# Query and gate transposes by DMA from DRAM in a hybrid retention and attention layer

## The chip, the core and the metric

The kernel runs on one core of one Trainium2 chip. Such a core has five engines that run side by side, each with its own list of instructions: TensorE (PE, the matrix engine), VectorE (DVE), ScalarE (ACT), GpSimd (POOL) and SyncE (SP). Here SP issues all transfers but one, in order, and sixteen DMA engines carry them out. SBUF is the memory on the core with 128 partitions, PSUM the banks that TensorE writes, DRAM the large memory outside. The metric is the device time of one execution in microseconds (us), lower is better.

## What is computed

One decoder layer, with x of 2048 tokens by 1024 channels, all in float32. After an RMS norm one projection gives the columns of two groups of heads and a gate for each group:

```python
h = rms_norm(x, norm_w)
rq, rk, rv, rg, sq, sk, sv, sg = split(h @ w_in)         # 256 256 512 512 512 128 128 512
# A: retention, 4 heads, chunks of 128 tokens
scores = (qc @ kc.T) * decay ;  intra = scores @ vc       # qc, kc with rotary phase
state = chunk_decay * state + (kc * zeta).T @ vc ;  cross = (qc * xi) @ state_before
ro = group_norm(intra + cross) * ret_norm_w * silu(rg)
# B: attention over a window of 128 keys, 8 query heads, 2 key heads
q, k = rms_norm(sq, q_norm_w), rms_norm(sk, k_norm_w)
logits = q @ kband.T / 8 + bias                           # the chunk's keys and the previous chunk's
so = softmax([logits, sink])[..., :-1] @ vband * silu(sg)
out = x + concat([ro, so]) @ w_out
```

## The kernel before, in words

The tokens are cut into 16 chunks of 128, taken as 8 pairs. The two projections run as four stages of block products: stage 1 gives the columns of sq, sk and sv, stage 2 those of rq, rk and rv, stage 3 the gates rg and sg, stage 4 is the output projection. Each stage forms, for each pair, a 2 by 2 block product in seven products in place of eight (the numbers 1 to 7 in `STEPS`), so that there are 4 x 7 x 8 = 224 products. Each float32 operand is split into a high and a low part (`split`: ACT makes the high part, DVE the low one), and a product is twelve matmuls, three for each of four slices of the inner dimension. They write the tiles called `acc`. TensorE's other results are called `m`.

Attention (`window`, `attend`, `values`) runs between the products of stages 2 and 3, a chunk at a time: load queries (`aq`) and keys (`akv`) from DRAM, multiply by their norm factors (`qn`, `kn`), transpose the key (`turn k`) and the four 128-column blocks of the queries (`turn q`) on TensorE against the identity (`ident`), copy them from PSUM on ACT (`ks`, `qT`), logits, softmax, four transposes of the weights for each key head (`turn weights`, `pT`), and for each pair of chunks the product with the values. The values are read from DRAM into `vn`, `vs` and `vd`, each of 128 partitions by four shifted runs of 128 columns, in quarters of 32 partitions. `retention` does the same for its heads. Both groups' outputs (`so`, `ro`) go to DRAM.

The gates (`gates`, `gate(n, c, ...)`: n = 0 for retention, 1 for attention, c the chunk) come from the products of stage 3. The gate of retention for an even chunk is put into DRAM (`g_dram`) and read back, at a due time of `GATE[0] + p * GATE[1]` for pair p; the others are used as they come. With n = 0 the output `go` is multiplied by the gate, transposed on TensorE in four blocks (`turn gated`, 16 chunks x 4) and copied back from PSUM on ACT (`mixed`). With n = 1 the gate itself is transposed by `turn_by_dma`, while `so` is already transposed. That function exists because the transposing DMA works on 16-bit elements: ACT first puts the low and the high half words of all 512 columns apart (`apart`, 1024 columns of uint16), SP issues a transposing DMA from SBUF to SBUF (`turned`), and ACT puts the halves together again. `go` then goes into stage 4 as an operand.

The order of the instructions is made by a planner, `Program.emit`, when the kernel is built. Each operation has a due time, counted in products, and costs for its engine (time taken, time to the result). The planner walks through time, takes for each engine the operation that can start first by these costs, and emits it. So on each engine, and on SP's list of transfers ("Q"), the order is fixed at build time, and on the chip an instruction waits at its place for what it needs; what stands behind it on that engine waits too. Buffers of 128 by 512 (tag `k`) are shared by all, in groups with a limit (`SHARE`; the group of `apart` and `turned` has 6).

Every operation is recorded through one helper, so all rows of the profile bear its line, L377, and are told apart by their tiles: `m<-ident,qn` are the query transposes, `m<-ident,go` those of the gated outputs, `m<-ident,kn` the keys', `m<-ks,qT` the logits, `acc<-w,x` the products.

Of the kernel before, what the change touches and what calls it, by code (L numbers as in the profile page):

```python
# [310 lines left out]
LOG = None  # L311


def dve(n, two=False, lat=0.08):
# [34 lines left out]
def dma(kb, issue=0.45):  # L349
    return {"Q": (0.45 + kb / 1024, 2.6, issue)}  # L350


# [28 lines left out]
def layer(ctx, tc, xt, xfirst, xtok, nw, w_in, w_rn, qkw, sinks, biasg, rope, dmask, gpow, w_out, out):  # L381
# [35 lines left out]

    def scratch(shape, name, n):
        t = dram.tile([n, *shape], F32, name=name)
        return [Buf(name=name, ap=t[i]) for i in range(n)]  # L420
# [13 lines left out]
    def store(dst, b, due, kbytes=256, of=lambda t: t):  # L434
        op(dma(kbytes), lambda e: e.dma_start(dst(), of(b())), [b], [dst], due, label=f"store {b.name}")

    def f(t):
# [384 lines left out]
    def retention(at):  # L822
# [4 lines left out]
        for c in range(NCH):  # L827
# [3 lines left out]
            v0, v1 = (Part(v, lambda t, s=s: t[:, s]) for s in (slice(0, 256), slice(256, 512)))  # L831
            load(a0, rq_dram[0][c], due - 3, 192, also=(a,))
            load(a1, rq_dram[1][c], due - 3, 64, also=(a,), of=lambda t: t[:, 0:128])
            load(rp, given(rope[c].rearrange("p s c -> p (s c)")), due - 3)
            load(v0, rq_dram[1][c], due - 3, 128, also=(v,), of=lambda t: t[:, 128:384])
            load(v1, aq_dram[1][c], due - 3, 128, also=(v,), of=lambda t: t[:, 256:512])
            for j, r in enumerate((rstd_all, rsq_all)):

                def go(e, rp=rp, j=j, r=r, c=c):
                    t = rp().rearrange("p (s c) -> p s c", s=2)[:, :, j * P : (j + 1) * P]  # L840
                    e.activation(t, t, AF.Copy, scale=r()[:, c : c + 1])

                op({"A": act(256, 0.09)}, go, [rp, r], [rp], due - 2, label="scale rope")

            tcos, tsin, qk = kb("tcos", "ret"), kb("tsin", "ret"), kb("qk", "ret")
            for i, t in enumerate((tcos, tsin)):

                def go(e, t=t, i=i, a=a, rp=rp):
                    h = "p (h c) -> p h c"
                    e.tensor_tensor(  # L850
                        t().rearrange(h, h=2),
                        a().rearrange(h, h=2),
                        rp().rearrange("p (s c) -> p s c", s=2)[:, i : i + 1, :].to_broadcast([P, 2, 256]),
                        ALU.mult,
                    )

                op(both(512), go, [a0, a1, rp], [t], due, label="rotary", also=(a,))

            for i, alu in enumerate((ALU.subtract, ALU.add)):
# [10 lines left out]

                op(both(256), go, [tcos, tsin], [qk], due + 0.1, label="rotary sum")

            pt, qkT = ps(), kb("qkT", "ret")

            def go(e, pt=pt, qk=qk):
                for i in range(4):
                    e.transpose(pt()[:, i * P : (i + 1) * P], qk()[:, i * P : (i + 1) * P], ident())

            op(turns(4), go, [qk, ident], [pt], due + 0.2, "small", label="turn qk")

            op({"A": act(512)}, lambda e, pt=pt, qkT=qkT: e.activation(qkT(), pt(), AF.Copy), [pt], [qkT], due + 0.3,
               label="qkT")
            halves = (slice(0, 64), slice(64, 128))
# [132 lines left out]
    def window(at):  # L1016
# [44 lines left out]
    def values_from(c, rows, part, whole, name, due):  # L1061


        first = c * P + rows
        source = [akv_dram[k] for k in range(-1, NCH) if first < (k + 2) * P and first + P > (k + 1) * P]
        src = akv_rows[first : first + P, 128:256].rearrange("(u p) d -> p u d", p=32)
        op(
            dma(64, 0.63), lambda e: e.dma_start(part().rearrange("p (u d) -> p u d", d=P), src), source, [part], due - 4,
            label="load " + name, also=(whole,),
        )  # L1070

    def values(c, held, due, d, differences):
# [4 lines left out]
        n, s = kb("vn", "att"), kb("vs", "att")  # L1077
        parts = []
# [5 lines left out]
        for k, (place, seen, whole) in enumerate(((differences[0], parts[0], n), (differences[3], parts[7], s))):  # L1084
            values_from(c + k, P, place, d, "vd", due)
            op(
                both(512), lambda e, place=place, seen=seen: e.tensor_tensor(place(), place(), seen(), ALU.subtract),
                [place, seen], [place], due + 1, label="vd", also=(d, whole),
            )
# [5 lines left out]
        def go(e):  # L1095
# [9 lines left out]
            for u in range(4):  # L1105
                for g, r in enumerate((L, H)):
                    for k, rows in enumerate((L, H)):
# [5 lines left out]
                        )  # L1113

        reads = [*parts, *differences, *held[0][0], *held[1][0], *held[0][2], *held[1][2]]
        op(f32(512, 3.2), go, reads, pavs, due + 2, "both", label="values", also=(n, s, d, *own))
        for k in range(2):
            so = kb("so", "att")
            op({"A": act(512)}, lambda e, so=so, k=k: e.activation(so(), pavs[k](), AF.Copy), [pavs[k]], [so], due + 2.1,
               label="so")  # L1120
            store(so_dram[c + k], so, due + 2.2)

# [45 lines left out]
    def attend(c, a, b, fac, facs, due, bias_t, ks_t, nsnk, held):  # L1168
# [11 lines left out]

        op(both(512), go, [a, facs], [qn], due, label="qn")

# [14 lines left out]

        def go(e):
            for i in range(4):
                e.transpose(pq()[:, i * P : (i + 1) * P], qn()[:, i * P : (i + 1) * P], ident())  # L1200

        op(turns(4), go, [qn, ident], [pq], due + 0.2, "small", label="turn q")
        qT = kb("qT", "att")

# [75 lines left out]
        for g in range(KVH):  # L1280
            pm, own = pms[g], owns[g]
            pp, pT = ps(), kb("pT", "att")

            def go(e, pp=pp, pm=pm):
                for j in range(GRP):
                    e.transpose(pp()[:, j * P : (j + 1) * P], pm()[:, j * P : (j + 1) * P], ident())

            op(
                turns(4), go, [*weights_of[g], *weights_of[2 + g], ident], [pp], due + 1.3 + 0.3 * g, "small",
                label="turn weights", also=(pm,),  # L1290
            )
            op({"A": act(512)}, lambda e, pT=pT, pp=pp: e.activation(pT(), pp(), AF.Copy), [pp], [pT], due + 1.4 + 0.3 * g,
               label="pT")

# [9 lines left out]

            op({"G": (0.61, 0.7, True)}, go, [pT], [part], due + 1.5 + 0.3 * g, label="own", also=(own,))
            pTs.append(pT)
# [15 lines left out]
    mixes = {}  # L1322

    def turn_by_dma(t, due):


        apart, turned = kb("apart", "turned"), kb("turned", "turned")
        words = lambda x: x.bitcast(U16).rearrange("p (c h) -> p h c", h=2)
        planes = lambda x: x.bitcast(U16).rearrange("p (h c) -> p h c", h=2)
        op(  # L1330
            {"A": act(1024)}, lambda e: e.activation(planes(apart()), words(t()), AF.Copy), [t], [apart], due,
            label="apart",
        )
        op(
            {"Q": (1.4, 3.0, 0.45)},
            lambda e: e.dma_start_transpose(
                turned().bitcast(U16).rearrange("p (j r) -> p j r", r=P), apart().bitcast(U16)
            ),
            [apart], [turned], due, label="turn by dma",
        )  # L1340
        op(
            {"A": act(1024)}, lambda e: e.activation(words(t()), planes(turned()), AF.Copy), [turned], [t], due + 0.1,
            label="together",
        )

    def gate(n, c, due, g):
# [14 lines left out]
        else:  # L1361
# [96 lines left out]
RET = (107.0, 2.8)  # L1458
GATE = (150.0, 1.2)

# [97 lines left out]
```

## Time and profile before

| | us |
|---|---|
| median of 3 runs (709.15 to 710.41) | 709.81 |
| the profiled execution, whole | 709.88 |
| its span, first to last instruction | 708.0 |
| PE busy | 702.2 |
| DVE busy | 606.9 |
| ACT busy | 471.9 |
| share of the sixteen DMA engines | 67.5% |

The profile is of one execution. A row of a group reads: line, engine, operation, tile written, tiles read, shape, count, then the busy time of all, the mean length of one in ns, and the time the engine stood idle ahead of them with what ended it. In a row of waits stand who waited, on what, the sum, how often and the longest. A row of issued transfers gives the destination, the source, the size and the time from issue to landing. "SPq" is SP's list of transfers. The tile views of a transfer give the time for which one instruction holds SP (shortest, median, longest) and its time to landing.

### The profile page before, as it was taken

What the parts mean: (1) busy time and instruction counts of PE and PEld (TensorE: products, weight loads), DVE (VectorE), ACT (ScalarE), POOL (GpSimd) and SP (SyncE); (2) the same over time, 40 slices, a digit from 0 to 9 for tenths busy, and PEclk for the clock granted to TensorE, in tenths of its full rate; (3) what the DMA queues carried; (4) which work ended last, traced back from release to release, by engine and by line L of the source; (5) the groups of instructions that cost most, each with busy time, mean ns of one, the idle gap of its engine ahead of it and who ended that gap; (6) DMA issues with size and microseconds to landing.
All of it is one profiled execution on the core that took longest, in us unless ns stands there. A gap on an engine that the chain in (4) does not pass through costs nothing.

```text
span 708.0 us, 15295 instructions
## 1 busy us (share of the span) xinstructions
PE 702.2 (99%) x5324; PEld 603.3 (85%) x5324; DVE 606.9 (86%) x1458; ACT 471.9 (67%) x1103; POOL 43.8 (6%) x75
## 2 busy tenths in 40 slices
PE   9999999999999999999999999999999999999998
PEld 7888888889999999998888888888888878888886
DVE  6999877877997977799999979998699989997862
ACT  7666966655795548788588667789999976250500
POOL 1000000025110001002001010000000000000000
PEclk9999999999999999999999999999999999999999
DMA  8978939968545557998977738292999951324722
GB/s 322 358 263 294 404 123 316 313 230 276 183 132 169 198 172 213 357 302 257 335 223 251 208 114 290 71 333 100 303 341 235 256 128 60 103 91 131 256 103 90
DMA packets 118924, 157.66 MB, mean 223 GB/s; under 512 B 28736, under 2 KB 57408, under 8 KB 118848
## 3 DMA queue, kind: packets, MB, share of 16 engines
q1 hardware_dynamic: 118704, 156.69, 67.5%
q8 instruction: 42, 0.69, 0.4%
q14 instruction: 34, 0.28, 0.1%
q10 hardware_dynamic: 144, 0.00, 0.0%
HBM read 110.44 MB, written 42.01 MB: 215 GB/s over the span
## 4 chain that ended last, share of the span: by engine, by line
PE 97%; DVE 2%; issue 0%; DMA 0%; SPq 0%; ACT 0%
PE acc L377 80%; PE m L377 17%; DVE w L377 1%; DVE x L377 1%; DVE t L377 0%; DMA res<-in_xtok 0%; DVE res L377 0%; DVE go L377 0%; SPq L377 0%; ACT x L377 0%; DVE none L377 0%
## 5 line engine op out<-in xcount | busy, mean ns | idle before, releaser
L377 PE MATMUL acc<-w,x 128*128 128x512 f32 (+1 forms) x2700 | 598.5, 378 | 1.1 <-DVE x L377 0.8
L377 PEld LDWEIGHTS acc<-w,x 128*128 128x128 f32 x2700 | 491.1, 188 | 82.0 <-issue 2.7
L377 DVE TENSOR_TENSOR x<-x 128x512 fp32r<-128x512 f32 (+2 forms) x220 | 145.4, 681 | 16.4 <-ACT x L377 15.9
L377 ACT ACTIVATE x<-x 128x512 fp32r<-128x512 f32 (+1 forms) x187 | 112.1, 617 | 7.0 <-DVE x L377 2.6
L377 ACT ACTIVATE w<-w 128x512 fp32r<-128x512 f32 (+1 forms) x72 | 41.2, 603 | 38.1 <-DMA w<-in_w_out 17.8
L377 DVE TENSOR_TENSOR w<-w 128x512 fp32r<-128x512 f32 (+3 forms) x96 | 62.5, 669 | 2.9 <-ACT w L377 2.9
L377 DVE TENSOR_TENSOR s<-acc,s 128x512 f32<-128x512 f32 (+1 forms) x64 | 42.0, 656 | 16.3 <-PE acc L377 15.8
L377 ACT ACTIVATE pm<-lg,nm 128x128 f32<-128x128 f32 x128 | 49.7, 392 | 6.8 <-DVE lg L377 6.8
L377 DVE CUSTOM_DVE_ANT_0 lg<-m,bias,nsnk 128x160 f32<-128x160 f32 x128 | 42.3, 381 | 10.1 <-PE m L377 10.0
L377 DVE SCALAR_TENSOR_TENSOR w<-w,nw_sb 128x512 fp32r<-128x512 f32 (+3 forms) x72 | 49.3, 706 | 0.9 <-ACT w L377 0.7
L377 POOL TENSOR_SCALAR_AFFINE_SELECT own<-pT 64x512 f32<-64x512 f32 x32 | 26.4, 837 | 291.7 <-ACT pT L377 246.5
L377 DVE TENSOR_TENSOR t<-acc,t 128x512 f32<-128x512 f32 (+2 forms) x33 | 21.1, 640 | 17.0 <-PE acc L377 16.6
L377 ACT ACTIVATE x<-go 128x512 fp32r<-128x512 f32 x40 | 24.0, 633 | 12.1 <-PE acc L377 6.3
L377 ACT ACTIVATE s<-acc 128x512 f32<-128x512 f32 (+1 forms) x32 | 18.2, 569 | 19.6 <-PE acc L377 14.7
L377 DVE TENSOR_TENSOR r<-acc,t 128x512 f32<-128x512 f32 (+1 forms) x32 | 21.0, 656 | 11.8 <-PE acc L377 11.4
L377 ACT ACTIVATE w<-w,nw_sb 128x512 fp32r<-128x512 f32 (+3 forms) x43 | 28.0, 681 | 2.7 <-DMA w<-in_w_in 2.7
L377 DVE TENSOR_TENSOR x<-go,x 128x512 fp32r<-128x512 f32 x40 | 27.2, 685 | 0.0
L377 ACT ACTIVATE ro<-ro,nmu,rg 128x128 f32<-128x128 f32 x64 | 25.1, 482 | 0.9 <-DVE nmu L377 0.9
L377 ACT ACTIVATE c<-acc 128x512 f32<-128x512 f32 (+1 forms) x24 | 13.4, 559 | 16.6 <-PE acc L377 13.9
L377 ACT ACTIVATION_READ_ACCUMULATOR pm<-lg,nm 128x1 f32 x128 | 24.4, 190 | 0.0
L377 DVE TENSOR_TENSOR t<-acc,s 128x512 f32<-128x512 f32 (+1 forms) x32 | 21.0, 656 | 3.3 <-PE acc L377 2.8
L377 ACT ACTIVATE xk<-xk 128x512 f32<-128x512 f32 x32 | 19.8, 620 | 5.3 <-DMA xk<-in_xtok 5.3
(133 smaller groups left out, 726.4 us busy)
## 6 DMA issues: line engine op xcount, KB each, us to landing
x<-in_xt SPq DMA_DIRECT2D x80, 256.0 KB, 5.0
x<-s_dram SPq DMA_DIRECT2D x64, 256.0 KB, 4.3
w<-in_w_in SPq DMA_DIRECT2D x40, 256.0 KB, 5.4
s_dram<-x SPq DMA_DIRECT2D x32, 256.0 KB, 5.0
xk<-in_xtok SPq DMA_DIRECT2D x32, 256.0 KB, 5.1
res<-in_xtok SPq DMA_DIRECT2D x32, 256.0 KB, 3.3
w<-in_w_out SPq DMA_DIRECT2D x20, 256.0 KB, 4.7
aq<-aq_dram SPq DMA_DIRECT2D x16, 256.0 KB, 4.8
```

The lines of the kernel that those rows point to most:

```text
L377: return lambda *a, **k: self.order.put(op(*a, **k))
```

## The change

Four things change.

- `turn_by_dma` goes through DRAM. ACT still puts the half words apart, but the result is stored to a DRAM tensor (`planes`), and the transposing DMA reads that tensor as 256 rows of 512 columns, so that row 2t is the low half words of token t and row 2t + 1 the high ones. What lands in SBUF then has the halves of each word side by side, and the second ACT pass is gone. Each turn is now a split on ACT, a store and a transposing DMA. All three stand in SP's and ACT's lists like everything else; the transposing DMA waits on SP for the store to land.
- All 16 query blocks are turned this way in place of four TensorE transposes and an ACT copy each. Their load and their normalisation are due two products earlier (`EARLIER_Q`).
- The gated outputs of retention of the 8 even chunks are turned this way, those of the odd chunks stay on TensorE. The 16 gates of attention, transposed by DMA before, use the new form. `GATE` goes from (150.0, 1.2) to (145.0, 2.0).
- The values load in five DMAs for a pair of chunks instead of ten: `vn` in one of 128 partitions, `vs` in one of 96 and one of 32, `vd` in two of 32 as before.

The sets "qk" and "weights" in `TURNED` are empty, so retention's transposes and those of the weights stay on TensorE, and `EARLIER_K` and `LATER_W` have no effect.

```diff
+TURN = (1.5, 3.0, 1.35)
+TURNED = {"q": range(NCH), "qk": (), "weights": (), "gated": range(0, NCH, 2)}
+EARLIER_Q, EARLIER_K, LATER_W = 2.0, 4.0, 4.0
...
+VALUES = {P: dma(256, 0.6), 96: dma(192, 0.6), 32: dma(64, 0.63)}
...
+    def turn_by_dma(t, to, planes, due, of=None, also=()):
+        apart = kb("apart", "turned")
+        op(
+            {"A": act(1024, 0.12)},
+            lambda e: e.activation(
+                apart().bitcast(U16).rearrange("p (h c) -> p h c", h=2),
+                t().bitcast(U16).rearrange("p (c h) -> p h c", h=2), AF.Copy,
+            ),
+            of or [t], [apart], due, label="apart", also=also,
+        )
+        store(planes, apart, due + 0.1, of=lambda t: t.bitcast(U16))
+        op(
+            {"Q": TURN},
+            lambda e: e.dma_start_transpose(
+                to().bitcast(U16).rearrange("p (j r) -> p j r", r=2 * P),
+                planes().rearrange("t (h c) -> (t h) c", h=2),
+            ),
+            [planes], [to], due + 0.2, label="turn by dma",
+        )
...
+    planes_dram = [scratch([P, 1024], f"planes{n}_dram", NCH, U16) for n in range(6)]
...
-            load(a, aq_dram[0][c], at(c) - 4)
+            load(a, aq_dram[0][c], at(c) - 4 - (EARLIER_Q if c in TURNED["q"] else 0))
...
-        src = akv_rows[first : first + P, 128:256].rearrange("(u p) d -> p u d", p=32)
+        at = akv_rows[first : first + n, 128:256]
+        src = bass.AP(at.tensor, at.offset, [[512, n], [32 * 512, 4], [1, P]])
...
-        for k, (t, starts) in enumerate(((n, (0, 32, 64, 96)), (s, (32, 64, 96, 0)))):
-            for r, rows in zip(QUARTERS, starts):
-                parts.append(Part(t, lambda t, r=r: t[r, :]))
-                values_from(c + k, rows, parts[-1], t, t.name, due)
+        parts = [Part(n, lambda t: t), Part(s, lambda t: t[0:96, :]), Part(s, lambda t: t[last, :])]
+        for k, t, rows, part, many in ((0, n, 0, parts[0], P), (1, s, 32, parts[1], 96), (1, s, 0, parts[2], 32)):
+            values_from(c + k, rows, part, many, t, t.name, due)
...
-        op(both(512), go, [a, facs], [qn], due, label="qn")
+        soon = due - (EARLIER_Q if c in TURNED["q"] else 0)
+        op(both(512), go, [a, facs], [qn], soon, label="qn")
...
-        op(turns(4), go, [qn, ident], [pq], due + 0.2, "small", label="turn q")
         qT = kb("qT", "att")
+        if c in TURNED["q"]:
+            turn_by_dma(qn, qT, planes_dram[2][c], soon + 0.1)
...
-        op({"A": act(512)}, lambda e: e.activation(qT(), pq(), AF.Copy), [pq], [qT], due + 0.35, label="qT")
...
-        if n == 0:
+        if n == 0 and c not in TURNED["gated"]:
...
         else:
-            turn_by_dma(g, due + 0.3)
+            t = (o, g)[n]
+            turn_by_dma(t, t, planes_dram[n][c], due + 0.3)
+        if n == 1:
             op(both(512), lambda e: e.tensor_tensor(o(), g(), o(), ALU.mult), [g, o], [o], due + 0.4, label="mixed")
...
-GATE = (150.0, 1.2)
+GATE = (145.0, 2.0)
```

More of the change, by code (lines that the diff above doesn't have):

```diff
@@ L416, in fixed, with scratch @@
         return Buf(name=name, ap=const.tile(shape, dtype, name=name))
-    def scratch(shape, name, n):
-        t = dram.tile([n, *shape], F32, name=name)
+    def scratch(shape, name, n, dtype=F32):
+        t = dram.tile([n, *shape], dtype, name=name)
         return [Buf(name=name, ap=t[i]) for i in range(n)]
@@ L831, in retention @@
             v0, v1 = (Part(v, lambda t, s=s: t[:, s]) for s in (slice(0, 256), slice(256, 512)))
-            load(a0, rq_dram[0][c], due - 3, 192, also=(a,))
-            load(a1, rq_dram[1][c], due - 3, 64, also=(a,), of=lambda t: t[:, 0:128])
-            load(rp, given(rope[c].rearrange("p s c -> p (s c)")), due - 3)
+            soon = due - (EARLIER_K if c in TURNED["qk"] else 0)
+            load(a0, rq_dram[0][c], soon - 3, 192, also=(a,))
+            load(a1, rq_dram[1][c], soon - 3, 64, also=(a,), of=lambda t: t[:, 0:128])
+            load(rp, given(rope[c].rearrange("p s c -> p (s c)")), soon - 3)
             load(v0, rq_dram[1][c], due - 3, 128, also=(v,), of=lambda t: t[:, 128:384])
@@ L841, in go @@
                     e.activation(t, t, AF.Copy, scale=r()[:, c : c + 1])
-                op({"A": act(256, 0.09)}, go, [rp, r], [rp], due - 2, label="scale rope")
+                op({"A": act(256, 0.09)}, go, [rp, r], [rp], soon - 2, label="scale rope")
             tcos, tsin, qk = kb("tcos", "ret"), kb("tsin", "ret"), kb("qk", "ret")
@@ L855, in go @@
                     )
-                op(both(512), go, [a0, a1, rp], [t], due, label="rotary", also=(a,))
+                op(both(512), go, [a0, a1, rp], [t], soon, label="rotary", also=(a,))
             for i, alu in enumerate((ALU.subtract, ALU.add)):
@@ L869, in go @@
                     )
-                op(both(256), go, [tcos, tsin], [qk], due + 0.1, label="rotary sum")
+                op(both(256), go, [tcos, tsin], [qk], soon + 0.1, label="rotary sum")
             pt, qkT = ps(), kb("qkT", "ret")
[L875 to L882, printed above, removed]
+            if c in TURNED["qk"]:
+                turn_by_dma(qk, qkT, planes_dram[3][c], soon + 0.1)
+            else:
+                def go(e, pt=pt, qk=qk):
+                    for i in range(4):
+                        e.transpose(pt()[:, i * P : (i + 1) * P], qk()[:, i * P : (i + 1) * P], ident())
+                op(turns(4), go, [qk, ident], [pt], due + 0.2, "small", label="turn qk")
+                op({"A": act(512)}, lambda e, pt=pt, qkT=qkT: e.activation(qkT(), pt(), AF.Copy), [pt], [qkT], due + 0.3,
+                   label="qkT")
             halves = (slice(0, 64), slice(64, 128))
@@ L1059, in window, with values_from @@
                 held = []
-    def values_from(c, rows, part, whole, name, due):
+    def values_from(c, rows, part, n, whole, name, due):
         first = c * P + rows
-        source = [akv_dram[k] for k in range(-1, NCH) if first < (k + 2) * P and first + P > (k + 1) * P]
-        src = akv_rows[first : first + P, 128:256].rearrange("(u p) d -> p u d", p=32)
+        source = [akv_dram[k] for k in range(-1, NCH) if first < (k + 2) * P and first + n + 96 > (k + 1) * P]
+        at = akv_rows[first : first + n, 128:256]
+        src = bass.AP(at.tensor, at.offset, [[512, n], [32 * 512, 4], [1, P]])
         op(
-            dma(64, 0.63), lambda e: e.dma_start(part().rearrange("p (u d) -> p u d", d=P), src), source, [part], due - 4,
+            VALUES[n], lambda e: e.dma_start(part().rearrange("p (u d) -> p u d", d=P), src), source, [part], due - 4,
             label="load " + name, also=(whole,),
@@ L1077, in values @@
         n, s = kb("vn", "att"), kb("vs", "att")
-        parts = []
-        for k, (t, starts) in enumerate(((n, (0, 32, 64, 96)), (s, (32, 64, 96, 0)))):
-            for r, rows in zip(QUARTERS, starts):
-                parts.append(Part(t, lambda t, r=r: t[r, :]))
-                values_from(c + k, rows, parts[-1], t, t.name, due)
-        for k, (place, seen, whole) in enumerate(((differences[0], parts[0], n), (differences[3], parts[7], s))):
-            values_from(c + k, P, place, d, "vd", due)
-            op(
-                both(512), lambda e, place=place, seen=seen: e.tensor_tensor(place(), place(), seen(), ALU.subtract),
-                [place, seen], [place], due + 1, label="vd", also=(d, whole),
+        last = QUARTERS[3]
+        parts = [Part(n, lambda t: t), Part(s, lambda t: t[0:96, :]), Part(s, lambda t: t[last, :])]
+        for k, t, rows, part, many in ((0, n, 0, parts[0], P), (1, s, 32, parts[1], 96), (1, s, 0, parts[2], 32)):
+            values_from(c + k, rows, part, many, t, t.name, due)
+        for k, place, of, rows, whole in ((0, differences[0], parts[0], QUARTERS[0], n), (1, differences[3], parts[2], last, s)):
+            values_from(c + k, P, place, 32, d, "vd", due)
+            op(
+                both(512),
+                lambda e, place=place, rows=rows, whole=whole: e.tensor_tensor(place(), place(), whole()[rows, :], ALU.subtract),
+                [place, of], [place], due + 1, label="vd", also=(d, whole),
             )
@@ L1113, in go @@
                         )
+        late = due + (LATER_W if c in TURNED["weights"] else 0)
         reads = [*parts, *differences, *held[0][0], *held[1][0], *held[0][2], *held[1][2]]
-        op(f32(512, 3.2), go, reads, pavs, due + 2, "both", label="values", also=(n, s, d, *own))
+        op(f32(512, 3.2), go, reads, pavs, late + 2, "both", label="values", also=(n, s, d, *own))
         for k in range(2):
             so = kb("so", "att")
-            op({"A": act(512)}, lambda e, so=so, k=k: e.activation(so(), pavs[k](), AF.Copy), [pavs[k]], [so], due + 2.1,
+            op({"A": act(512)}, lambda e, so=so, k=k: e.activation(so(), pavs[k](), AF.Copy), [pavs[k]], [so], late + 2.1,
                label="so")
-            store(so_dram[c + k], so, due + 2.2)
+            store(so_dram[c + k], so, late + 2.2)
     def qk_sums(p, row, col, b, due):
@@ L1196, in attend, with go @@
         )
-        def go(e):
-            for i in range(4):
-                e.transpose(pq()[:, i * P : (i + 1) * P], qn()[:, i * P : (i + 1) * P], ident())
-        op(turns(4), go, [qn, ident], [pq], due + 0.2, "small", label="turn q")
         qT = kb("qT", "att")
+        if c in TURNED["q"]:
+            turn_by_dma(qn, qT, planes_dram[2][c], soon + 0.1)
+        else:
+            def go(e):
+                for i in range(4):
+                    e.transpose(pq()[:, i * P : (i + 1) * P], qn()[:, i * P : (i + 1) * P], ident())
+            op(turns(4), go, [qn, ident], [pq], due + 0.2, "small", label="turn q")
+            op({"A": act(512)}, lambda e: e.activation(qT(), pq(), AF.Copy), [pq], [qT], due + 0.35, label="qT")
         def go(e):
@@ L1282, in attend, with go @@
             pp, pT = ps(), kb("pT", "att")
[L1284 to L1293, printed above, removed]
+            if c in TURNED["weights"]:
+                turn_by_dma(pm, pT, planes_dram[4 + g][c], due + 1.3 + 0.3 * g, [*weights_of[g], *weights_of[2 + g]], (pm,))
+            else:
+                def go(e, pp=pp, pm=pm):
+                    for j in range(GRP):
+                        e.transpose(pp()[:, j * P : (j + 1) * P], pm()[:, j * P : (j + 1) * P], ident())
+                op(
+                    turns(4), go, [*weights_of[g], *weights_of[2 + g], ident], [pp], due + 1.3 + 0.3 * g, "small",
+                    label="turn weights", also=(pm,),
+                )
+                op({"A": act(512)}, lambda e, pT=pT, pp=pp: e.activation(pT(), pp(), AF.Copy), [pp], [pT], due + 1.4 + 0.3 * g,
+                   label="pT")
             r = (L, H)[slot]
@@ L1303, in go @@
                 )
-            op({"G": (0.61, 0.7, True)}, go, [pT], [part], due + 1.5 + 0.3 * g, label="own", also=(own,))
+            op({"G": (0.61, 0.7, True)}, go, [pT], [part], due + 1.5 + 0.3 * g + (LATER_W if c in TURNED["weights"] else 0), label="own", also=(own,))
             pTs.append(pT)
@@ L1322, in layer @@
     mixes = {}
[L1324 to L1344, printed above, removed]
     def gate(n, c, due, g):
```

## The prediction

> **What bounds the kernel now.** I read the page first: the busy lines, the granted clock and the chain that ended last.
>
> ```profile
> span 708.0 us, 15295 instructions
> ...
> PE 702.2 (99%) x5324; PEld 603.3 (85%) x5324; DVE 606.9 (86%) x1458; ACT 471.9 (67%) x1103; POOL 43.8 (6%) x75
> ...
> PEclk9999999999999999999999999999999999999999
> ...
> q1 hardware_dynamic: 118704, 156.69, 67.5%
> ...
> PE 97%; DVE 2%; issue 0%; DMA 0%; SPq 0%; ACT 0%
> ```
>
> TensorE is busy all the time at the full granted clock and carries 97% of the chain. A busy PE may still be a waiting one, so the waits of PE and of its weight loads come next, and those of the one DMA queue, SP's.
>
> ```profile
> PE m L377 <- DVE none L377: 1.3, 1, 1.3
> PE acc L377 <- DVE x L377: 0.8, 1, 0.8
> PE acc L377 <- ACT x L377: 0.2, 1, 0.2
> ```
> ```profile
> SPq L377 <- ACT so L377: 44.6, 6, 16.1
> ```
>
> Beyond the start-up (1.3 us), PE waits 1.0 us in the whole run. So whatever leaves PE's list shortens the run, as long as nothing arrives later than now. SP's queue, in contrast, stands still for long times (once 16.1 us behind one store) and PE does not notice. How full the other resources are differs by stretch (window, sum, then busy time of PE, PEld, DVE, ACT, POOL, the clock, the DMA engines' share, GB/s):
>
> ```profile
> 150.00:350.00 200.00, 200.00 (x2184) 186.65 (x2183) 172.99 (x530) 137.18 (x403) 27.95 (x39) 1.00 0.73 239
> 350.00:450.00 100.00, 100.00 (x1081) 84.18 (x1080) 92.21 (x294) 74.87 (x204) 6.39 (x8) 1.00 0.68 214
> 450.00:510.00 60.00, 60.00 (x537) 50.04 (x536) 49.23 (x138) 53.33 (x113) 1.45 (x2) 1.00 0.58 200
> 510.00:570.00 60.00, 60.00 (x290) 49.89 (x289) 56.88 (x94) 59.21 (x83) 0.00 (x0) 1.00 0.99 278
> 570.00:630.00 60.00, 58.94 (x258) 47.84 (x257) 58.09 (x97) 31.70 (x54) 0.00 (x0) 1.00 0.31 97
> ```
>
> Attention and retention lie in 150 to 510; the gates' sixteen transposing DMAs run from 508.6 to 571.3 (row below). From 510 to 570 four resources are full together: PE, ACT (59.21 of 60), DVE (56.88) and the DMA engines (0.99). That is the tight place.
>
> **The change, part by part.** *TensorE loses* 16 groups of four query transposes and 8 of the 16 groups of gated outputs. A matmul's own duration is not its price, as they overlap; the price stands in the time line (start, length) and the chain.
>
> ```profile
> 245.77 0.27 PE L377 MATMUL m<-ident,kn 128*128 128x128 f32 x1
> 245.88 0.60 PE L377 MATMUL m<-ident,qn 128*128 128x128 f32 x4
> 246.24 6.52 PE L377 MATMUL acc<-w,x 128*128 128x384 f32 x36
> ...
> 367.12 0.94 PE L377 MATMUL acc<-w,x 128*128 128x512 f32 x3
> 367.90 0.27 PE L377 MATMUL m<-ident,kn 128*128 128x128 f32 x1
> 367.92 3.00 PE L377 MATMUL acc<-w,x 128*128 128x512 f32 x12
> 370.76 0.60 PE L377 MATMUL m<-ident,qn 128*128 128x128 f32 x4
> ...
> 537.18 0.60 PE L377 MATMUL m<-ident,go 128*128 128x128 f32 x4
> ...
> 540.39 0.60 PE L377 MATMUL m<-ident,go 128*128 128x128 f32 x4
> ```
> ```profile
> 540.99 10.92 PE acc L377 x48
> ```
>
> A key transpose with the query group behind it takes 246.24 - 245.77 = 0.47 us until the next product; a key transpose alone 367.92 - 367.90 = 0.02. The query group is worth 0.45. A gated group with twelve products takes 540.39 - 537.18 = 3.21 us, twelve products alone 12 x 10.92 / 48 = 2.73; the lone group is worth 0.48, one beside others less, so 0.45 again. 24 x 0.45 = 10.8 us leave PE.
>
> *TensorE's order shifts.* In the order of the changed program the groups of small tiles stand in more pieces: weight transposes in 29 instead of 26, logits 19 instead of 17, and one more piece each of retention's transposes, outputs and updates: 8 more entries. The lone key transpose prices one: 370.76 - 367.12 = 3.64 for fifteen products (15 x 0.2275 = 3.41) and the transpose, that is 0.23, about 0.11 of it its own (245.88 - 245.77). So 0.12 an entry: +1.0 us. The logits stay where they were among the products (first chunk before the 63rd, last before the 143rd, both orders); retention's last chunk comes after product 158, not 148, so its gates are nearer to the last stage, which begins after 168 (counted with the late arrivals below).
>
> *ACT:*
>
> ```profile
> L377 ACT ACTIVATE x<-x 128x512 fp32r<-128x512 f32 x180 | 109.5, 625 | 6.6 <-DVE x L377 2.6 <-DVE w L377 1.8 <-DMA out<-res 0.9
> L377 DVE TENSOR_TENSOR x<-x 128x512 fp32r<-128x512 f32 x180 | 123.2, 692 | 16.3 <-ACT x L377 15.9
> L377 PE MATMUL m<-ident,qn 128*128 128x128 f32 x64 | 9.6, 272 | 0.0
> L377 ACT ACTIVATE qT<-m 128x512 f32<-128x512 f32 x16 | 9.5, 594 | 7.0 <-PE m L377 6.9
> L377 ACT ACTIVATE go<-m 128x512 f32<-128x512 f32 x16 | 9.3, 608 | 0.7 <-PE m L377 0.5
> L377 ACT ACTIVATE t<-turned 128x1024 uint16<-128x1024 uint16 x8 | 11.1, 1387 | 0.0
> L377 ACT ACTIVATE apart<-t 128x1024 uint16<-128x1024 uint16 x8 | 8.5, 1080 | 0.1
> ```
>
> 24 more splits into half words x 1.08 = 25.9; gone are 16 x 0.594 = 9.5, 8 x 0.608 = 4.9 and the 16 joins x 1.39 = 22.2. That is -18.5 at the gates, the full stretch, and +7.8 in the attention, where ACT has room (137 of 200). On the path: nothing; without that room the query's way would be longer by the 0.5 us that a split takes over a copy. DVE's work is unchanged. POOL's too; it waits for the transposed weights, which stay on PE.
>
> *Moved:* the gates that are read back start five products earlier and two products apart, so their loads, SiLU, multiplication and store go from the full stretch into 450 to 510, where ACT has 53 of 60, DVE 49 and the DMA engines 0.58. Nothing, while that holds; if not, see the DVE rival.
>
> *DMA and SP:*
>
> ```profile
> L377 SPq DMA_TRANSPOSE turned<-apart x16: 1232/1321/1889, 508.6 to 571.3; - x16
> ...
>   DVE x L377: 1.9, 1
> ...
> DMA to landing us min/median/max: 3.0/4.4/5.8
> ```
> ```profile
> L377 SPq DMA_DIRECT2D so_dram<-so x16: 319/320/1247, 205.4 to 496.9; - x16
> ...
> DMA to landing us min/median/max: 2.0/4.1/5.2
> ```
> ```profile
> s_dram<-x SPq DMA_DIRECT2D x32, 256.0 KB, 5.0
> ...
> x<-s_dram SPq DMA_DIRECT2D x64, 256.0 KB, 4.3
> ...
> vn<-aq_dram SPq DMA_DIRECT2D x32, 64.0 KB, 4.4
> ...
> vd<-aq_dram SPq DMA_DIRECT2D x16, 64.0 KB, 2.1
> ```
>
> Added: 40 stores and 24 transposing DMAs; the values lose 40 of their 80 loads with the same bytes. SP issues 40 x 0.32 + 24 x 1.32 - 40 x 0.32 = 32 us more, spread over 500. The DMA engines moved 156.69 MB in 0.675 x 708 = 478 us, so a plain 0.262 MB takes 0.8 us of all sixteen. In 510 to 570 they moved 278 x 60 = 16.7 MB in 59 us; the 16 transposes are 4.2 MB, the other 12.5 at 0.328 MB/us take 38 us, which leaves 21 / 16 = 1.3 us a transpose (estimate). Added: 40 x 0.8 + 24 x 1.3 = 63 us, so 541 of some 700, a share of 0.77. By stretch: 16 queries, 34 us on the 214 of 300 in 150 to 450; gates, 30 us on 113 of 180 in 450 to 630. It fits if spread.
>
> A transpose that reads DRAM does not occur in the trace. Its issue lies between a store's 0.32 and 1.89, the longest row; its landing between 2.1 and 5.8. I take 1.32 and 4.4, the same instruction from SBUF. The query's way from its normalisation grows from 0.45 + 0.59 = 1.0 to 1.08 + 4.1 + 4.4 = 9.6 us. The code starts it two products earlier (224 products of twelve matmuls in some 700 us: 3.1 us each), and the order keeps the logits seven products behind the key's transpose (56 to 63): covered, by a few us only. If a landing is late, the logits stop PE. Before, a transposed gate came late once (1.9 us on DVE x), and PE's only wait of 0.8 was on DVE x. 0.8 for 16 transposes makes 2.0 for 40: +1.2 us; the bounds are 0 and 24 x (5.8 - 4.4) = 34 with no cover at all.
>
> Values: a matmul group now waits for whole tiles; loads are four products ahead, which hides 4.4 as it hid it. Without that, one pair would wait some 2 us (4.4 against 2.1).
>
> **Sum,** against the profiled 709.88 (0.07 over the median of 709.81): 709.88 - 10.8 + 1.0 + 1.2 = 701.3 us.
>
> The Trainium skill speaks against the change: "VectorE: DVE Perf Modes", section "The three transpose paths", gives 390 ns for a 128x128 transpose on TensorE and 1309 ns through the DMA crossbar, and advises TensorE where PSUM will do. By its 390 the 96 transposes would be worth 37 us and the time 672 (estimate); the rows say 272 ns each and 0.45 us for four, so the trace disagrees by this overlap.
>
> **Rivals.** *SP's queue stands still (slower).* A transposing DMA waits on SP for the store just issued, and product loads stand behind. In the changed order 4 pairs are 2 apart, one 3, six 4. At 4.1 us landing and 0.32 an issue SP stops 4 x 3.8 + 3.5 + 6 x 3.1 = 37 us. A product's load is planned 2.5 products ahead, 7.8 us; landing 4.3, split 0.63 and 0.69 leave 2.2 of cover, 24 for eleven. 13 us reach PE: 701.3 + 13 = 714; at a landing of 5.0, 724. It decides from 8.6 us on (the sum's gain), that is landings of 3.7. Against it: the 16.1 us stop above cost PE nothing, as the loads needed had gone before. The Trainium skill ("DMA: Bandwidth & Descriptors", "Two DMAs through the same engine are not ordered") asks for this wait on the completion; no run here shows it left out.
>
> *The DMA engines are over-full in the gates.* The 14 or so turns that stay in 510 to 570 bring 14 x 0.8 = 11 us into a stretch at 0.99. If the last stage waits for all of it: 701.3 + 11 = 712. For it: the share. Against: gated outputs now start earlier, and 25 and 41 us are free on both sides.
>
> *DVE takes over.* DVE's work is the same in less time. In 350 to 450 it has 92 of 100, in 510 to 570 57 of 60. If the some 9 groups removed there bring nothing: +4, 705.
>
> *All of it, and more:* no new waits, and the 1.0 that PE waits now goes with ACT's relief: 698.
>
> **How the numbers follow.** The forecast 0.52 (its own range 699 to 704), DVE 0.17, all 0.08: faster 0.77. DMA over-full 0.12, of which 0.05 within 0.2%; SP 0.11: slower 0.18. 0.2% is about what a measurement here can tell. The range 697 to 712 leaves out most of the SP rival.
>
> **What would show it.** Right: no PE rows with qn, 32 with go, PE busy near 691, waits of PE under 4 us, DMA share near 0.77. Wrong: PE waiting for DMA qT or for x behind SP's waits on planes; transposes landing over 6 us; ACT or DVE waiting for DMA go, r or t at 500 to 580.

## The result and the profile after

The changed kernel takes 698.96 us (median of 4 runs, 698.44 to 699.53) against 709.48 for the kernel before in the same comparison (4 runs). The ratio is 0.985, 95% interval 0.9833 to 0.9867, so 10.5 us are gone. Forecast were 701.3. The profiled execution took 699.53.

The page of the changed kernel, the same rows as before:

```profile
span 697.8 us, 15132 instructions
...
PE 693.0 (99%) x5228; PEld 592.9 (85%) x5228; DVE 602.6 (86%) x1458; ACT 464.3 (67%) x1087; POOL 41.0 (6%) x75
...
q1 hardware_dynamic: 149168, 173.47, 78.9%
...
PE 97%; DVE 2%; issue 0%; ACT 0%
```

TensorE has 96 matmuls fewer and is still the chain. Its waits, all of them, and two of SP's:

```profile
PE m L388 <- DVE none L388: 1.3, 1, 1.3
```
```profile
SPq L388 <- DMA planes_dram<-apart: 25.7, 13, 4.5
SPq L388 <- ACT so L388: 23.8, 6, 11.4
```

The 1.0 us for which PE waited in the run before (beyond the 1.3 us at the start) is gone, and no wait has taken its place. SP stands still 13 times for a store of half words to land, 25.7 us in sum, and PE does not notice. The transposing DMAs that read DRAM (time on SP, then time to landing, from the view of the tile `qT`; of all 40, the longest landing was 7.0 us, that of a gate, `r`), and the stores:

```profile
L388 SPq DMA_TRANSPOSE qT<-planes_dram x16: 1232/1264/1758, 160.4 to 402.5; - x16
...
DMA to landing us min/median/max: 3.2/4.5/6.7
```
```profile
planes_dram<-apart SPq DMA_DIRECT2D x40, 256.0 KB, 4.5
```

The stretches (columns as before):

```profile
150.00:350.00 200.00, 199.87 (x2149) 184.44 (x2148) 177.44 (x542) 144.54 (x407) 26.00 (x41) 1.00 0.91 273
350.00:450.00 100.00, 100.00 (x1072) 82.54 (x1071) 92.39 (x297) 79.90 (x207) 5.90 (x8) 1.00 0.76 238
450.00:510.00 60.00, 60.00 (x514) 50.07 (x516) 47.91 (x114) 52.86 (x101) 1.45 (x2) 1.00 0.89 271
510.00:570.00 60.00, 60.00 (x305) 49.72 (x298) 53.61 (x106) 48.66 (x84) 0.00 (x0) 1.00 1.02 299
570.00:630.00 60.00, 60.00 (x267) 49.67 (x266) 60.00 (x101) 26.10 (x46) 0.00 (x0) 1.00 0.40 120
```

ACT has come down from 59 to 49 of 60 in the gates, the DMA engines are at 1.02 there, DVE is full from 570 to 630. PE is busy everywhere.

### The profile page after: what moved, and what is told of

It reads as the page before. It is cut to its first block, busy times and chain, and to the rows that moved or that the text cites. A ratio compares the mean times of both kernels' runs of the same rounds, so it can differ in the third digit from the quotient of the medians.

```text
span 697.8 us, 15132 instructions
## 1 busy us (share of the span) xinstructions
PE 693.0 (99%) x5228; PEld 592.9 (85%) x5228; DVE 602.6 (86%) x1458; ACT 464.3 (67%) x1087; POOL 41.0 (6%) x75
## 4 chain that ended last, share of the span: by engine, by line
PE 97%; DVE 2%; issue 0%; ACT 0%
PE acc L388 82%; PE m L388 16%; DVE lg L388 1%; DVE x L388 0%; DVE w L388 0%; DVE vd L388 0%; DVE qn L388 0%; ACT x L388 0%; ACT pT L388 0%; DVE kn L388 0%; DVE t L388 0%; DVE none L388 0%; DVE nm L388 0%; DVE rden L388 0%; DVE es L388 0%
## 5 line engine op out<-in xcount | busy, mean ns | idle before, releaser
L388 DVE TENSOR_TENSOR x<-x 128x512 fp32r<-128x512 f32 (+2 forms) x220 | 145.5, 682 | 16.8 <-ACT x L388 16.1
L388 ACT ACTIVATE pm<-lg,nm 128x128 f32<-128x128 f32 x128 | 49.8, 393 | 14.8 <-DVE lg L388 11.6
L388 POOL TENSOR_SCALAR_AFFINE_SELECT own<-pT 64x512 f32<-64x512 f32 x32 | 24.7, 782 | 277.8 <-ACT pT L388 229.6
L388 ACT ACTIVATE apart<-qn 128x1024 uint16<-128x1024 uint16 x16 | 16.9, 1057 | 14.0 <-DVE qn L388 14.0
```

Of the source, the lines that this page charges most:

```text
L388: return lambda *a, **k: self.order.put(op(*a, **k))
```

## The experiments

The theory to be tested is that TensorE alone sets the time, and what leaves its list is what the run gains. The rivals on record: SP's list stands still, the DMA engines are over-full in the gates, DVE takes over. Twelve kernels were run, all as variants of the changed kernel. In the traces put_back and twice keep the order of every engine; adjacent keeps TensorE's and moves a few operations of DVE and ACT; gated_all_thin keeps the order of gated_all, but for twelve stores more. In all the others the planner made a new order, which is then part of what the run measures.

| run | us (median) | ratio to the kernel before, 95% interval |
|---|---|---|
| the change | 698.96 | 0.985 (0.9833 to 0.9867) |
| put_back | 704.81 | 0.9937 (0.9919 to 0.9955) |
| q_only | 702.92 | 0.991 (0.9891 to 0.9929) |
| neither | 708.38 | 0.9975 (0.9962 to 0.9988) |
| adjacent | 771.24 | 1.0863 (1.0828 to 1.0899) |
| twice | 750.37 | 1.0576 (1.0538 to 1.0613) |
| gated_all | 716.39 | 1.0091 (1.0072 to 1.011) |
| gated_all_thin | 719.35 | 1.0128 (1.0106 to 1.015) |
| qk_half | 704.71 | 0.992 (0.9902 to 0.9938) |
| qk_all | 700.69 | 0.9878 (0.9858 to 0.9897) |
| qk_first8 | 703.98 | 0.9917 (0.99 to 0.9933) |
| values_ten | 713.62 | 1.0048 (1.0032 to 1.0064) |
| gate_old | 703.32 | 0.9898 (0.9882 to 0.9914) |

The kernel before was run again beside each of three groups of runs: 709.62 us beside put_back, q_only, neither and adjacent, 709.67 beside twice, gated_all, qk_half and qk_all, and 710.2 beside the rest.

### What a group of transposes costs TensorE

```diff
-            turns(1), lambda e: e.transpose(pk()[:, 0:P], kn(), ident()), ...
+        def go(e):
+            for i in (1, 2, 3, 1, 0):
+                e.transpose(pk()[:, i * P : (i + 1) * P], kn(), ident())
+            turns(1), go, ...
```

> The changed kernel with 64 more TensorE transposes: behind each of the 16 key transposes stand four that nobody reads, where the query transposes stood before. All engines' orders stay as they are. If TensorE alone sets the time, all of the group's price comes back: 16 x 0.45 = 7.2 us, 706.2 us. If another engine (DVE, or the DMA engines) has become the bound in places, part is hidden: under 703.

It came to 704.81, 5.85 us more than the change. One such place in the time line of this kernel and of the changed one:

```profile
245.06 0.71 PE L388 MATMUL m<-ident,kn 128*128 128x128 f32 x5
245.53 2.70 PE L388 MATMUL acc<-w,x 128*128 128x384 f32 x14
```
```profile
243.34 0.27 PE L388 MATMUL m<-ident,kn 128*128 128x128 f32 x1
243.37 2.85 PE L388 MATMUL acc<-w,x 128*128 128x384 f32 x15
```

0.47 against 0.03: a group of four is worth 0.44 us on PE, 7.0 for sixteen; the time lines show 0.43 to 0.45 at each of the sixteen places. 5.85 of it reached the end, nearer to the 7.2 of TensorE as the bound than to the 4 or less of the rivals; the interval of the ratio is 1.3 us to either side. The time lines also show where the rest went. The two profiled spans differ by 5.2 us: put_back's first group starts 0.7 us earlier (156.6 against 157.3 us), and between the groups it was 1.2 us shorter in three stretches (191 to 215, 258 to 279 and 363 to 386 us of the changed kernel). In the first, TensorE's weight loads wait for an operand from DVE, 0.45 us in the change and 0.20 in put_back; in the other two, 64 matmuls of the logits took 1.34 us in put_back and 1.75 in the change, and why is open. So what another engine hid of the 7.0 us is small.

```diff
-TURNED = {"q": range(NCH), ..., "gated": range(0, NCH, 2)}
+TURNED = {"q": range(NCH), ..., "gated": ()}
```

> The changed kernel with all 16 gated outputs of retention on TensorE again, queries and gates as in the change. TensorE as the bound: 8 x 0.45 = 3.6 us back, 702.6. DMA engines over-full in the gates: the 8 stores and 8 transposing DMAs cost about what the TensorE groups saved, 699 or less.

702.92: 4.0 us back, as TensorE's account has it (3.6).

```diff
-TURNED = {"q": range(NCH), ..., "gated": range(0, NCH, 2)}
+TURNED = {"q": (), ..., "gated": ()}
```

> The changed kernel with queries and gated outputs on TensorE again; what is left of the change is the gates' way through DRAM without a second ACT pass, the values in five loads and the gates' due times. TensorE as the bound: 24 x 0.45 = 10.8 us back, 709.8; 708.8 if the 1.0 us for which TensorE waited before went with ACT's relief. If the values' loads or the gates' new form bring time by themselves: 706 or less.

708.38: 9.4 us back. Forecast were 708.8, if PE's 1.0 us of waits before went with ACT's second pass; in this run PE waits for nothing but the start. What it keeps of the change (the gates' new form, the values in five DMAs, the due times) makes it faster than the kernel before by 1.2 us in the medians, 0.25% (0.12 to 0.38) in the ratio. So nearly all of the gain comes with the 24 groups that leave TensorE's list.

### How much room SP's list has

```diff
-        store(planes, apart, due + 0.1, ...)
+        op(dma(256), lambda e: None, [apart], [planes], due + 0.1, ...)
...
-            lambda e: e.dma_start_transpose(...)
+            lambda e: [e.dma_start(planes(), apart().bitcast(U16)), e.dma_start_transpose(...)]
```

> The changed kernel with each store of half-word planes moved down SP's list to just ahead of its transposing DMA (all 40), the rest of all orders unchanged. SP then stands still for a whole landing, 4.5 us, 40 times. By the rival's rule (2.2 us of cover for each stop) 40 x 2.3 = 92 us reach TensorE: 791. If SP's list runs well ahead of need, as the long stops before suggest, a few us: 700 to 706.

771.24, far from the 700 to 706 of my own theory and nearer to the rival's 791. SP's waits and the longest of PE's:

```profile
SPq L388 <- DMA planes_dram<-apart: 156.1, 40, 6.3
```
```profile
PE acc L388 <- ACT s L388: 18.2, 4, 6.8
PE acc L388 <- ACT x L388: 12.9, 4, 6.9
```

156.1 us of stops less 2.2 us of cover for each of the 40 are 68; the run lost 72. That the two are so near is partly luck. PE's waits beyond the start sum to 47 us in this run, not 68; the other 24 are busy time of PE (717.4 us against 693.0 for the same matmuls), which ran at a lower clock after its stops (0.83 from 570 to 630; last section). By the same rule the 13 stops of the changed kernel, 2.0 us on average, stay below the cover, though the longest, 4.5, does not. So the rival's mechanism is real: 26 us of stops cost nothing that the profile shows, 156 us cost 72. Where between them it begins to cost, no run here shows.

```diff
-            lambda e: e.dma_start_transpose(to()..., planes()...),
+            lambda e: [e.dma_start_transpose(x..., planes()...) for x in (to(), idle())],
```

> The changed kernel with every transposing DMA issued twice, the second into a tile that nobody reads; TensorE's, DVE's and ACT's orders unchanged. The DMA engines get 40 x 1.3 = 52 us more work (share 0.79 to 0.86), SP 40 x 1.26 = 50 us more. If the DMA engines and SP have room: under 701. If the gates' stretch is at their limit, as their share of 1.0 there says, the 20 or so turns there bring 26 us late: 708 or more.

750.37: 51 us more, as much as SP's 50 or the DMA engines' 52. Most of it is lost from 510 on (windows of this kernel):

```profile
510.00:570.00 60.00, 50.05 (x247) 39.78 (x246) 40.78 (x85) 40.77 (x72) 0.00 (x0) 0.91 1.03 283
570.00:630.00 60.00, 46.15 (x187) 36.23 (x185) 37.53 (x60) 26.07 (x41) 0.00 (x0) 0.91 1.03 251
```

The gates' stretch has no room for twice the turns. Whether the bytes or SP's time are short, this run cannot tell.

```diff
-TURNED = {"q": range(NCH), ..., "gated": range(0, NCH, 2)}
+TURNED = {"q": range(NCH), ..., "gated": range(NCH)}
```

> The changed kernel with the gated outputs of all 16 chunks turned by DMA, not of 8. TensorE as the bound: another 8 x 0.45 = 3.6 us off, 695.4. DMA engines over-full in the gates: no gain or a loss, 699 to 705.

716.39: instead of 3.6 us off, 17.4 on, beyond both expectations. The kernel before is faster. TensorE's time line and the window (this kernel):

```profile
582.01 3.17 PE L388 MATMUL acc<-w,x 128*128 128x512 f32 x12 [1.31 <-ACT s L388]
592.14 0.80 PE L388 MATMUL acc<-w,x 128*128 128x512 f32 x1 [6.97 <-ACT w L388]
596.48 3.78 PE L388 MATMUL acc<-w,x 128*128 128x512 f32 x8 [3.54 <-DVE w L388]
```
```profile
570.00:630.00 60.00, 45.81 (x178) 35.69 (x177) 49.45 (x81) 15.40 (x27) 0.00 (x0) 0.86 0.62 177
```

PE waits for weights of the output projection. Six of their loads stand together in SP's list; first in this kernel, then in the changed one:

```profile
583.03 3.70 SPq L388 DMA_DIRECT2D w<-in_w_out  x6
```
```profile
565.40 3.90 SPq L388 DMA_DIRECT2D w<-in_w_out  x6
```

They stand 16 places further down, behind the eight stores and eight transposing DMAs more, and leave 18 us later. SP does not stand still longer for that: from 505 us until these loads leave, all its waits sum to 16.0 us in this kernel and to 18.1 in the changed one. Those for half words, in the same order:

```profile
SPq L388 <- DMA planes_dram<-apart: 0.8, 3, 0.3
```
```profile
SPq L388 <- DMA planes_dram<-apart: 3.5, 2, 3.2
```

The time in which SP was issuing grew instead, from 60.4 - 18.1 = 42 to 78.0 - 16.0 = 62 us. The next run takes away most of the stores' bytes:

```diff
-TURNED = {"q": range(NCH), ..., "gated": range(0, NCH, 2)}
+TURNED = {"q": range(NCH), ..., "gated": range(NCH)}
...
-        store(planes, apart, due + 0.1, of=lambda t: t.bitcast(U16))
+        op(dma(256), lambda e: e.dma_start(planes()[:, 0:128], apart().bitcast(U16)[:, 0:128]), ...)
...
+        t = dram.tile([4, P, 1024], U16, name=f"planes{n}_dram")
+        planes_dram.append([Buf(name=f"planes{n}_dram", ap=t[i % 4]) for i in range(NCH)])
```

> The kernel with all 16 gated outputs by DMA (716.4), whose stores of half-word planes move only an eighth of their bytes (the rest of the planes holds zeros that 12 stores put there once, so what is turned is wrong); every list keeps its order but for those 12 on SP. SP's issues and waits for landings stay. If the bytes on the DMA engines are what is too much in the gates' stretch, some 24 stores there give back 24 x 0.7 = 17 us: 697 to 702. If it is SP's time and its stops for landings: 712 or more.

719.35. With an eighth of the stores' bytes nothing is won, and the same loads leave at the same time; the second row is PE's longest wait:

```profile
583.10 4.30 SPq L388 DMA_DIRECT2D w<-in_w_out  x6
```
```profile
PE acc L388 <- ACT w L388: 6.3, 1, 6.3
```

The share of the DMA engines from 510 to 570 fell from 1.12 to 0.99. This kernel has a cost of its own: it goes round four tensors of half words, and SP waits 11.6 us for transposing DMAs into `r`, `go` and `t` (0.4 in gated_all), which may hide a part of a gain. But the 17 us that were expected of the bytes are not there. So the stores' bytes alone are not what is too much in the gates. What is left is SP's list, by the sums above its issues and its order rather than its stops, and the transposing DMAs' own time on the DMA engines, which this run leaves as it is. The runs do not separate these.

```diff
...
-        for k, t, rows, part, many in ((0, n, 0, parts[0], P), (1, s, 32, parts[1], 96), (1, s, 0, parts[2], 32)):
-            values_from(c + k, rows, part, many, t, t.name, due)
+        for k, (t, starts) in enumerate(((n, (0, 32, 64, 96)), (s, (32, 64, 96, 0)))):
+            for r, rows in zip(QUARTERS, starts):
+                parts.append(Part(t, lambda t, r=r: t[r, :]))
+                values_from(c + k, rows, parts[-1], t, t.name, due)
...
```

> The changed kernel with the values in ten loads a pair again, 40 more DMAs of the same bytes in all. If SP has room there, as the prediction took it: 698.5 to 700. If SP's list is near its limit in the attention: 702 or more.

713.62: 14.7 us more than the change, by 40 more DMAs with the same bytes. They stand in the attention, but PE loses time mainly in the gates, long after (window and waits of this kernel):

```profile
510.00:570.00 60.00, 55.94 (x255) 45.74 (x254) 48.36 (x98) 47.27 (x93) 0.00 (x0) 0.97 1.03 287
570.00:630.00 60.00, 54.70 (x287) 44.18 (x286) 58.69 (x97) 28.14 (x49) 2.02 (x2) 0.97 0.56 153
```
```profile
PE m L388 <- DVE go L388: 3.2, 1, 3.2
PE acc L388 <- ACT x L388: 3.2, 1, 3.2
PE acc L388 <- DVE x L388: 3.0, 3, 1.8
```

With ten loads the turns bring a loss against the kernel before, with five a gain; in neither, where queries and retention's outputs stay on TensorE, the five loads and all else that is left bring 1.2 us. But this edit also lets the planner make another order, and how much of the 14.7 is that, and not the loads, is open.

```diff
-GATE = (145.0, 2.0)
+GATE = (150.0, 1.2)
```

> The changed kernel with the due times of the gates that are read back as before: (150.0, 1.2) for (145.0, 2.0), so that eight stores and eight transposing DMAs go from 450 to 510 us towards the full stretch. If the prediction's nothing for this move holds: 698.5 to 700. If the gates' stretch is at the limit, 8 x 2.1 = 17 us of the DMA engines more there: 705 or more.

703.32, 4.4 us more: between the two expectations. The earlier gates, with the order that the planner makes for them, are part of the gain; the stretch ahead of the gates (450 to 510, this kernel) now shows waits of PE.

```profile
450.00:510.00 60.00, 58.58 (x467) 47.95 (x466) 47.39 (x129) 51.10 (x96) 0.00 (x0) 1.00 0.87 255
```

### More turns in the retention

```diff
-TURNED = {"q": range(NCH), "qk": (), ...}
+TURNED = {"q": range(NCH), "qk": range(0, NCH, 2), ...}    # qk_half; range(NCH): qk_all; range(8): qk_first8
```

> The changed kernel with retention's queries and keys of the 8 even chunks also turned by DMA, their rotary steps four products earlier. TensorE as the bound: another 8 x 0.45 = 3.6 us off, 695.4. If the DMA engines (0.91 in 150 to 350 us) or the longer way to the scores stop TensorE: 699 to 705.

> As the run with the even chunks, but all 16 chunks' queries and keys of retention by DMA. TensorE as the bound: 7.2 us off, 691.8. Otherwise 699 to 712; the retention's state is handed from chunk to chunk, so that late landings would add up.

> The changed kernel with retention's queries and keys of the first 8 chunks by DMA, so that the added turns lie before the gates' stretch. TensorE as the bound: 8 x 0.44 = 3.5 us off, 695.4. If what the added transfers push back reaches the gates' stretch all the same, as in the run with the even chunks: 700 or more.

704.71, 700.69 and 703.98: TensorE has less to do each time, and none is faster than the change. The page's busy line and PE's waits of qk_all:

```profile
PE 688.2 (99%) x5164; PEld 587.5 (84%) x5164; DVE 605.0 (87%) x1458; ACT 468.0 (67%) x1086; POOL 44.3 (6%) x75
```
```profile
PE m L388 <- DVE sT L388: 2.1, 3, 1.0
PE acc L388 <- DVE x L388: 1.9, 3, 1.4
PE m L388 <- DVE none L388: 1.3, 1, 1.3
PE acc L388 <- ACT x L388: 0.8, 1, 0.8
```

PE is busy 4.8 us less than in the change (693.0) and waits for late operands instead. In qk_half the waits lie behind 540 us, in qk_first8 between 280 and 380. Why all 16 chunks cost less than 8 is open; each set has an order of its own. By the medians none of the twelve beats the change; the interval of qk_all overlaps the change's own.

## Why the prediction was right, and where it was not

**TensorE is the bound, and its list is the gain: right.** The change has no query transposes, 32 gated ones, and the chain is TensorE's before and after. The price of a group, 0.45 us from the time line, measured 0.44, and the two runs that put groups back cost 4.0 (forecast 3.6) and 9.4 (10.8, less 1.0 for waits that are gone). The 390 ns that the prediction quotes from the Trainium skill ("VectorE: DVE Perf Modes") are given there for bf16, while these transposes are float32, and the advice stands there in the section "Rules for kernel authors".

**The more pieces in TensorE's order, +1.0: not measured by itself.** The groups and the pieces together were to take 10.8 - 1.0 = 9.8 us off PE's busy time; it fell by 9.2 (702.2 to 693.0). Which of the two terms is off by these 0.6, no run tells.

**Late arrivals, +1.2: the term that was mis-sized.** PE's waits for late operands measured 0, and the 1.0 us of waits before went as well. The profiled span fell by 10.2 us (708.0 to 697.8): 9.2 of busy time and this 1.0. So the two errors on waits make 2.2 us, of which the busy time takes 0.6 back; most of the rest of the 2.3 us between the forecast and the median is that the profiled execution (699.53) was 0.6 above the median. Transposing DMAs for the queries land after 4.5 us, up to 6.7 (taken: 4.4, bounds 2.1 to 5.8, so the upper one was too low), and hold SP for 1.26 us (taken: 1.32). A landing of over 6 us was on record as a sign of being wrong; it came, and PE has no wait on `qT`: the seven products between key and logits covered it.

**ACT: right in direction.** 18.5 us fewer were forecast for the gates; from 450 to 630, with the gates that moved, ACT's busy time fell by 16.6 (in 510 to 570 from 59.2 to 48.7). The run neither, which has the joins gone and the rest on TensorE, has no waits of PE left; that ACT's relief alone removed them is not shown, as the values and the due times are changed there too.

**The DMA engines' share of 0.77: right in size** (0.789). Over-full gates by the stores' bytes: against it stands the thin run. Over-full by the transposing DMAs themselves no run excludes for the kernels with more turns; in the change, the share of 1.02 there left PE without a wait.

**SP has room, so that 32 us more cost nothing: true for this kernel, but for a thinner reason than given.** I took the 16.1 us stop that cost nothing for a sign that SP's list runs far ahead. The adjacent run shows that it does not: stops of some 4 us, 40 times, cost 72 us. A long stop tells only that nothing needed stood behind it at that place. The rival's 37 us of stops in eleven pairs were 25.7 in thirteen, which by its own rule stays within the cover; its mechanism was not absent.

**Values in five loads, and the gates moved: each priced at nothing, and that does not hold in the company of the turns.** Undone, they cost 14.7 and 4.4 us, a new order of the planner included. I had priced them one by one in the profile before, where SP had room. That in the changed kernel they make the room which the turns take fits these runs, but is not shown apart from the order.

**DVE takes over: no.** It is full from 570 to 630 (60.0 of 60) and PE waits for it nowhere after the start.

## What to carry to other kernels

When an engine is busy all the time and waits for nothing, price what leaves it by the starts of its neighbours in the time line, not by the lengths of the instructions; the sum then holds, as long as the room elsewhere does. Room in a queue that issues in order is not the share of time in which it is idle, and one long stop without harm does not prove it: put a stop or an extra issue into the kernel as it is after the change and measure. Parts of an edit that look free may be what the others need: undone, two such parts cost 14.7 and 4.4 us here. So price them together.

## What the runs showed of the hardware

TensorE's clock falls when it is left without work. In gated_all PE waits 6.97 and 3.54 us around 592; in the window behind, the granted clock (the third column from the end) is half, and eight matmuls of 512 columns take 3.78 us, 0.47 each, where a run of 48 in the profile before took 0.23 each.

```profile
560.00:580.00 20.00, 20.00 (x90) 16.58 (x89) 12.39 (x20) 4.61 (x8) 0.00 (x0) 1.00 1.16 256
580.00:592.00 12.00, 3.86 (x16) 2.33 (x14) 8.17 (x14) 3.84 (x7) 0.00 (x0) 0.82 1.06 326
592.00:600.00 8.00, 4.31 (x9) 3.13 (x10) 8.00 (x14) 4.34 (x8) 0.00 (x0) 0.50 0.95 260
600.00:610.00 10.00, 10.00 (x43) 8.16 (x42) 8.27 (x15) 1.79 (x3) 0.00 (x0) 0.93 0.23 79
```

The first of these waits began when the last matmul before it ended, at 582.01 + 3.17 = 585.18; a mean of 0.82 from 580 to 592 means half the clock for the last 4.3 us of that window, that is from 587.7 on, 2.5 us later. So a stop costs more than its length, which adds to the losses of adjacent, twice and gated_all. The Trainium skill ("TensorE: Matmul & The Clock Gate", section "Why this matters for your kernels") says that idle gaps of more than some 3 us bring the clock down to half. The half is what this trace shows, 0.50; the 3 us are not a safe bound here, as a shorter wait was enough in qk_half (PE's time line, then windows):

```profile
562.20 10.18 PE L388 MATMUL acc<-w,x 128*128 128x512 f32 x36 [2.09 <-ACT x L388]
```
```profile
560.00:562.20 2.20, 0.11 (x2) 0.00 (x1) 2.14 (x4) 2.20 (x5) 0.00 (x0) 1.00 1.20 238
562.50:565.90 3.40, 3.40 (x9) 2.31 (x8) 3.40 (x7) 3.28 (x6) 0.00 (x0) 0.50 1.37 197
```

A transposing DMA that reads DRAM took SP about as long as one that reads SBUF (medians of 1.26 and 1.32 us) and landed as fast (4.5 and 4.4 us), as the prediction took it.
